# A 90-degree rotation of an 8192 x 8192 matrix: twelve macro tiles as a loop, another buffer rotation, another split of the copies

## The chip, the cores and the metric

The kernel runs on one core of one Trainium2 chip. The metric is the device time of one execution in microseconds: the median over several runs. Profiles come from one further execution, taken by the hardware profiler; its span runs from the first to the last instruction.

## The reference: what is computed

```python
def setup_inputs():
    return {"x": np.random.randn(8192, 8192).astype(np.float32), "k": 1}

def reference(x, k):
    return np.rot90(x, k)
```

With k = 1, out[i, r] = x[r, 8191 - i]: a transposition with the order of the columns reversed. 268 MB are read and 268 MB are written, and nothing is calculated.

## The kernel before, in words

**Tiles.** The matrix is cut into KK = 16 macro tiles of R = 1024 rows by W = 4096 columns. A macro tile is read in T = 8 loads of 128 rows (2 MB each; load m is tile t = m % 8 of macro tile kk = m // 8), and written in J = 8 stores of 2 MB (output n is chunk j = n % 8 of macro tile kk = n // 8). So there are 128 loads and 128 outputs.

**Buffers.** Five buffers of 2 MB: LAND = 2 take turns for landing loads, OUTS = 3 for outputs (`out_buf`, lines 161 to 168). Between them stands `ring`, which holds one macro tile. Load n + 8 overwrites the places in the ring that output n was read from.

**Stages of one period.** SP issues the loads (`by_sync`). VectorE *turns* each landed load (`by_vector`, line 359): it writes it into the ring with reversed columns, the chunks that TensorE will transpose by a plain copy, the others by a transpose of 32 x 32 blocks. An output is then made in one of two ways. By TensorE (`by_pe`, lines 84 to 87: chunks 0 and 4 of most macro tiles, all chunks of the first and the last): 32 transposes into PSUM, in three parts, and ScalarE copies the parts to the output buffer (line 449). Or as a *moved* output: the sixteen 32-row pieces (`pairs`, line 264) are copied from the ring to their places by three engines: VectorE the first BY_DVE = 1 (line 341), GpSimd the next BY_POOL = 9 (line 324), ScalarE the last 6 (lines 430 and 439). 81 outputs are moved. ScalarE issues all the stores (line 457).

**What sets the order.** Every engine's program is written out by hand and runs straight through; semaphores tie them together:
- `room_for(wait, n)`: whoever writes output n waits until the last store from the same output buffer has landed. For a TensorE output it is TensorE that waits, before the last transpose of the first part (line 404).
- VectorE, before it turns load m, makes its piece of output m - 8 (line 340), waits for the load, and then for `s_pool` (GpSimd has made its last piece of output m - 8, line 346) or `s_half` (TensorE has transposed it, line 348).
- GpSimd waits for ScalarE's pieces before its eighth copy of an output and for VectorE's before its ninth (line 320), so that its last copy tells that the output is whole; ScalarE waits for that and issues the store (line 441).
- `taken`: a landing buffer is free when its load has been turned, and for the last load of a macro tile when TensorE has transposed the corner too (line 393; that stands after the second part of chunk 0).

Of the kernel before, what the change touches and what calls it, by code (L numbers as in the profile page):

```python
# [6 lines left out]
P = 128  # L7
# [6 lines left out]
J = W // (G * P)  # L14
# [5 lines left out]
SLOTS = T * J - 1  # L20

Q = 32
BY_DVE = 1
BY_POOL = 9
BY_PE = [0, 4]
EARLY = range(T + 2)
# [5 lines left out]
LAND = 2  # L32
OUTS = 3

LINE = 1024
HEAD = 224


def whole_reads(nc):

    for fn in nc.m.functions:
        for block in fn.blocks:
            for n, ins in enumerate(block.instructions):
                if not isinstance(ins, mybir.InstDMACopy):
                    continue
                src = ins.ins[0]
                ap = [list(d) for d in src.ap]
                if len(ap) == 3 and ap[2][0] == 1 and ap[1][0] == ap[2][1]:
                    ap = [ap[0], [1, 1], [1, ap[1][1] * ap[2][1]]]
                    block.instructions[n] = copy.replace(  # L50
                        ins,
                        ins=[copy.replace(src, ap=ap)],
                        ant_dge_precooked=False,
                    )


def slot(kk, t, j):
# [4 lines left out]
def kernel(tc: tile.TileContext, x: bass.AP, k: bass.AP, out: bass.AP):  # L62
# [93 lines left out]
    def load_buf(m):  # L156
        if m < T:
            return m % (LAND + OUTS)
        return LAND + 2 if m == T else (m - T - 1) % LAND

    def out_buf(n):
        e = n - (KK * J - J)
        if e < 0:
            return LAND + (n + 1) % OUTS
        ends = [load_buf(n_load - 2)]
        ends += [LAND + (KK * J - J + i + 1) % OUTS for i in range(OUTS)]
        ends += [load_buf(n_load - 1)]
        return ends[e % len(ends)]

    def once(e):  # L170
        seen = {}

        def wait(sem, n):
            if seen.get(sem, 0) < n:
                seen[sem] = n
                e.wait_ge(sem, n)

        return wait
# [51 lines left out]
    def at(v, first, dims):  # L230
        return bass.AP(
            tensor=v.tensor, offset=v[:, first : first + 1].offset, ap=[v.ap[0], *dims]
        )
# [29 lines left out]

    pairs = [(a, q) for a in range(P // Q) for q in range(P // Q)]

    def load(e, m):
        r0, c0 = macros[m // T]
        b = load_buf(m)
        rows = slice(0, P)
        if m in BOTH:  # L270
            rows = slice(0 if e is nc.sync else 1, P, 2)
        r = r0 + m % T * P
        e.dma_start(  # L273
            out=bufs[b][rows, :], in_=x[r : r + P, c0 : c0 + W][rows, :]
        ).then_inc(s_land[b], 16)

    def queues(m):
        if m in BOTH:
            return [nc.sync, nc.scalar]
        return [nc.scalar if m in EARLY and m % 2 else nc.sync]  # L280

    def load_in_turn(e, m):
        if e not in queues(m):
            return
        last = [i for i in range(m) if load_buf(i) == load_buf(m)]
        taken(e.wait_ge, last[-1])
        load(e, m)

    def landings(m):
        return 16 * sum(1 + (i in BOTH) for i in range(m + 1) if load_buf(i) == load_buf(m))  # L290
# [5 lines left out]
    with tc.tile_critical():  # L296
        for m in range(LAND + OUTS):
            for e in queues(m):
                load(e, m)
    tc.close()  # L300
    tc.compile()  # L301

    def by_gpsimd(e):
        e.memset(ident, 0.0).then_inc(s_id, 1)  # L304
        e.wait_ge(s_id, 1)
        e.affine_select(  # L306
            out=ident,
            in_=ident,
            compare_op=mybir.AluOpType.not_equal,
            fill=1.0,  # L310
            base=0,
            pattern=[[-1, P]],
            channel_multiplier=1,
        ).then_inc(s_id, 1)
        wait = once(e)
        for n, (kk, _, js, _) in enumerate(outs):
            if moved[n]:
                room_for(wait, n)
                wait(s_rev, turned_in(n))
                others = {BY_POOL - 2: s_act, BY_POOL - 1: s_dve}  # L320
                for c, (to, of) in enumerate(moves(n, pairs[BY_DVE : BY_DVE + BY_POOL])):
                    if c in others:
                        wait(others[c], moved_until(n))
                    i = e.tensor_copy(out=to, in_=of)  # L324
                i.then_inc(s_pool, 1)

    def by_sync(e):
        for m in range(LAND + OUTS, n_load):
            load_in_turn(e, m)

    def by_vector(e):
        wait = once(e)
        for m in range(n_load):
            kk, t = divmod(m, T)
            b = load_buf(m)
            n = m - T
            if n >= 0 and moved[n]:
                room_for(wait, n)
                wait(s_rev, turned_in(n))
                for to, of in moves(n, pairs[:BY_DVE]):  # L340
                    i = e.tensor_copy(out=to, in_=of)  # L341
                i.then_inc(s_dve, 1)
            e.wait_ge(s_land[b], landings(m))
            if n >= 0:
                if moved[n]:
                    e.wait_ge(s_pool, moved_until(n))  # L346
                else:
                    e.wait_ge(s_half, turned_until(n))
            for js in pieces[m]:
                if (m, js[0]) == (n_load - 1, J - 1):  # L350
                    e.wait_ge(s_half, turned_until(KK * J - J))
                if kk < KK - 1 and (t, js[0]) == (T - 1, J - 1):
                    wait(s_rev, rev[m, 0])
                    e.tensor_copy(  # L354
                        out=at(bufs[b][:], 0, [[CH, 1], [1, CH]]), in_=landed(b, js)
                    ).then_inc(s_rev, 1)
                    continue
                turn = e.transpose if in_quadrants(kk, js[0]) else e.tensor_copy
                turn(out=chunk(kk, t, js), in_=landed(b, js)).then_inc(s_rev, 1)  # L359
# [10 lines left out]
                yield n, parts[n]  # L370

    def by_tensor(e):
        wait = once(e)
        e.wait_ge(s_id, 2)
        used = {}
        for n, some in in_turn():
            kk, ts, js, blocks = outs[n]
            rows = len(ts) * P
            order = [(part, f) for part in some for f in part[2]]
            if js[0] == 0 and kk < KK - 1:  # L380
                late = parts[n][-1]
                order.sort(key=lambda o: (o[0] == late, o[1] % rows, o[1]))
            last = dict(order)
            for part, f in order:
                _, h, cols = part
                j, off = blocks[f // rows]
                t = ts[f % rows // P]
                if kk < KK - 1 and js[0] == 0 and f == parts[n][-1][2][0]:
                    m = kk * T + T - 1
                    wait(s_rev, rev[m, J - 1])  # L390
                    wait(s_freed, kk)
                    for g in range(G):
                        i = e.transpose(  # L393
                            corner[:, g * P : g * P + P],
                            bufs[load_buf(m)][:, g * P : g * P + P],
                            ident,
                        )
                    i.then_inc(s_corner, 1)
                if n == KK * J - J and h:
                    wait(s_freed, KK - 1)  # L400
                if used.get(h, part) != part:
                    wait(s_ev, evicted[used[h][0]] + 1)
                wait(s_rev, rev[kk * T + t, j])
                if part == parts[n][0] and f == last[part] and n != FIRST[1]:
                    room_for(wait, n)
                to = cols.index(f) * P
                i = e.transpose(  # L407
                    ps[h][:, to : to + P],
                    chunk(kk, t, [j])[:, 0, off : off + P],
                    ident,  # L410
                )
                if f == last[part]:
                    i.then_inc(s_half, 1)
                    used[h] = part

    def by_scalar(e):
        wait = once(e)
        e.wait_ge(s_id, 2)
        e.copy(scratch, ident[:, :1])  # L419
        for m in EARLY[LAND + OUTS :]:  # L420
            load_in_turn(e, m)
        for n, (kk, ts, js, blocks) in enumerate(outs):
            r0, c0 = macros[kk]
            rows = len(ts) * P
            b = out_buf(n)
# [16 lines left out]
            else:  # L442
                for k, h, cols in parts[n]:
# [11 lines left out]
            top = M - c0 - js[0] * CH - groups * P  # L455
            left = r0 + ts[0] * P
            e.dma_start(  # L457
                out=out[top : top + groups * P, left : left + rows].rearrange(
                    "(g m) f -> m g f", m=P
                ),  # L460
                in_=bufs[b][:, : groups * rows].rearrange("m (g f) -> m g f", f=rows),
            ).then_inc(s_store[b], 16)

    by_gpsimd(nc.gpsimd)
    by_sync(nc.sync)
    by_vector(nc.vector)
    by_tensor(nc.tensor)
    by_scalar(nc.scalar)

    last = {out_buf(n): n for n in range(n_out)}  # L470
    for b in sorted(last, key=last.get):
# [36 lines left out]
```

## Time and profile before

| what | value |
|---|---|
| time, median of 3 runs | 1258.23 us (1258.2 to 1258.35) |
| span of the profiled execution | 1256.9 us |
| HBM read, written | 268.44 MB, 268.44 MB |
| busy: GpSimd, ScalarE, VectorE, TensorE | 805.0, 682.5, 612.7, 330.0 us |
| store, issue to landing (median) | 18.6 us |
| load from SP, issue to landing (median) | 15.2 us |

The profiled execution's own time is its span of 1256.9 us; the median of the timed runs lies 1.33 us above it. How to read it: each engine has a row of busy time, and the DMA engines have a row of their own with the rate in GB/s for 40 equal slices of the span. A group of instructions is told as "line engine operation out<-in shape xcount | busy us, mean ns | idle before it and what ended the idle time"; the engines are PE (TensorE), DVE (VectorE), ACT (ScalarE), POOL (GpSimd) and SP. The queues q1 and q10 carry loads and stores, q8 and q14 carry instructions.

### The profile page before, as it was taken

What the parts mean: (1) busy time and instruction counts of PE and PEld (TensorE: products, weight loads), DVE (VectorE), ACT (ScalarE), POOL (GpSimd) and SP (SyncE); (2) the same over time, 40 slices, a digit from 0 to 9 for tenths busy, and PEclk for the clock granted to TensorE, in tenths of its full rate; (3) what the DMA queues carried; (4) which work ended last, traced back from release to release, by engine and by line L of the source; (5) the groups of instructions that cost most, each with busy time, mean ns of one, the idle gap of its engine ahead of it and who ended that gap; (6) DMA issues with size and microseconds to landing.
All of it is one profiled execution on the core that took longest, in us unless ns stands there. A gap on an engine that the chain in (4) does not pass through costs nothing.

```text
span 1256.9 us, 5389 instructions
## 1 busy us (share of the span) xinstructions
PE 330.0 (26%) x1556; PEld 267.9 (21%) x1556; DVE 612.7 (49%) x373; ACT 682.5 (54%) x637; POOL 805.0 (64%) x735
## 2 busy tenths in 40 slices
PE   1555122221122211222212322023220232214374
PEld 0444111211112110121201212012120121103364
DVE  2544554556545555455555555555555555453310
ACT  0334565565555655566555555556555655556454
POOL 0000886768867679677797767977678776795500
PEclk9987555555555555565555555555555555555588
DMA  9999999999999999999999999999999999999999
GB/s 398 420 431 428 430 428 430 430 430 430 428 429 430 430 429 428 430 429 430 429 430 429 430 427 431 430 430 429 430 429 430 429 429 429 429 430 429 430 426 394
DMA packets 36957, 537.22 MB, mean 427 GB/s; under 512 B 4160, under 2 KB 4160, under 8 KB 4160
## 3 DMA queue, kind: packets, MB, share of 16 engines
q10 hardware_dynamic: 19184, 278.93, 52.2%
q1 hardware_dynamic: 17744, 257.96, 48.0%
q8 instruction: 12, 0.20, 0.1%
q14 instruction: 17, 0.14, 0.0%
HBM read 268.44 MB, written 268.44 MB: 427 GB/s over the span
## 4 chain that ended last, share of the span: by engine, by line
DMA 72%; DVE 16%; POOL 5%; ACT 3%; issue 2%; PE 1%; ACTq 0%; SPq 0%; DVEq 0%
DMA buf<-in_x_dram 65%; DVE ring L359 16%; DMA out_dram<-buf 7%; POOL buf L324 5%; ACT buf L449 3%; PE ps L407 1%; ACTq L457 0%; DVE buf L341 0%; PE ps L393 0%; SPq L273 0%; DVE buf L354 0%; DVEq L346 0%; SPq L301 0%; SPq L193 0%; SPq L296 0%
## 5 line engine op out<-in xcount | busy, mean ns | idle before, releaser
L324 POOL COPY buf<-ring 32x1024 f32<-32x1024 f32 (+1 forms) x729 | 804.3, 1103 | 380.3 <-DMA out_dram<-buf 343.4
L407 PE MATMUL ps<-head,ring 128*128 128x128 f32 x1496 | 316.8, 384 | 880.6 <-DVE ring L359 430.3
L407 PEld LDWEIGHTS ps<-head,ring 128*128 128x128 f32 x1496 | 257.6, 200 | 936.9 <-DVE ring L359 435.0
L359 DVE COPY ring<-buf 128x1024 f32<-128x1024 f32 (+5 forms) x152 | 158.1, 1047 | 599.3 <-DMA buf<-in_x_dram 578.1
L439 ACT COPY buf<-ring 32x1024 f32<-32x1024 f32 (+1 forms) x405 | 414.8, 1024 | 4.9
L359 DVE STREAM_TRANSPOSE ring<-buf 128x3072 f32<-128x3072 f32 (+2 forms) x125 | 357.8, 2870 | 0.0
L449 ACT COPY buf<-ps 128x2048 f32<-128x2048 f32 (+1 forms) x134 | 174.6, 1355 | 251.8 <-PE ps L407 177.1
L430 ACT COPY buf<-ring 32x1024 f32<-32x1024 f32 x81 | 82.9, 1024 | 291.6 <-POOL buf L324 229.9
L341 DVE COPY buf<-ring 32x1024 f32<-32x1024 f32 x81 | 108.0, 1334 | 0.0
L393 PE MATMUL ps<-head,buf 128*128 128x128 f32 x60 | 16.2, 424 | 30.3 <-DVE buf L354 30.3
L393 PEld LDWEIGHTS ps<-head,buf 128*128 128x128 f32 x60 | 10.6, 213 | 35.7 <-DVE buf L354 35.7
L433 ACT COPY buf<-ps 128x512 f32<-128x512 f32 x15 | 8.8, 586 | 8.9 <-DMA out_dram<-buf 8.8
L354 DVE COPY buf<-buf 128x512 f32<-128x512 f32 x15 | 5.8, 388 | 0.0
L419 ACT ACT_TABLE_LOAD x1 | 1.3, 1283 | 3.4 <-PEq L301 3.4
L304 POOL MEMSET head<- 128x128 f32 x1 | 0.2, 205 | 2.9 <-POOLq L301 2.9
L306 POOL TENSOR_SCALAR_AFFINE_SELECT head<-head 128x128 f32<-128x128 f32 x1 | 0.3, 292 | 0.2 <-POOL head L304 0.2
L489 POOL MEMSET const-float32-0.0<- 128x1 f32 x1 | 0.1, 98 | 0.2 <-issue 0.2
L419 ACT COPY head<-head 128x1 f32<-128x1 f32 x1 | 0.2, 192 | 0.0
L489 POOL MEMSET const-bfloat16-1.0<- 128x1 bf16 x1 | 0.1, 100 | 0.0
L489 POOL MEMSET const-uint8-127<- 128x1 uint8 x1 | 0.1, 100 | 0.0
L489 POOL MEMSET const-float32-1.0<- 128x1 f32 x1 | 0.1, 98 | 0.0
## 6 DMA issues: line engine op xcount, KB each, us to landing
out_dram<-buf ACTq DMA_DIRECT2D x128, 2048.0 KB, 18.6
buf<-in_x_dram SPq DMA_DIRECT2D x121, 2048.0 KB, 15.2
buf<-in_x_dram ACTq DMA_DIRECT2D x3, 2048.0 KB, 17.3
buf<-in_x_dram SPq DMA_DIRECT2D x4, 1024.0 KB, 16.1
buf<-in_x_dram ACTq DMA_DIRECT2D x4, 1024.0 KB, 16.5
```

Of the source, the lines that this page charges most:

```text
L324: i = e.tensor_copy(out=to, in_=of)
L341: i = e.tensor_copy(out=to, in_=of)
L354: e.tensor_copy(out=at(bufs[b][:], 0, [[CH, 1], [1, CH]]), in_=landed(b, js)).then_inc(s_rev, 1)
L359: turn(out=chunk(kk, t, js), in_=landed(b, js)).then_inc(s_rev, 1)
L393: i = e.transpose(corner[:, g * P : g * P + P], bufs[load_buf(m)][:, g * P : g * P + P], ident,)
L407: i = e.transpose(ps[h][:, to : to + P], chunk(kk, t, [j])[:, 0, off : off + P], ident,)
L419: e.copy(scratch, ident[:, :1])
L430: e.copy(to, of)
L433: e.copy(at(bufs[b][:], rows - P, [[rows, G], [1, P]]), at(corner, 0, [[P, G], [1, P]]),).then_inc(s_freed, 1)
L439: i = e.copy(to, of)
L449: e.copy(at(bufs[b][:], cols[0], [[rows, deep], [1, run]]), at(ps[h][:], 0, [[run, deep], [1, run]]),).then_inc(s_ev, 1)
L489: nc = _bacc.Bacc("TRN2", target_bir_lowering=False, num_devices=1)
```

## The change

Three constants and tables change. VectorE makes the first 3 of the 16 pieces of a moved output and ScalarE the last 4, where it was 1 and 6; GpSimd keeps 9, but others than before. The output buffer of output n comes from the table TURN, which repeats after sixteen outputs, and no longer from (n + 1) % 3, which would not repeat with an even number of macro tiles. Within a macro tile a buffer still comes back after three outputs; where two macro tiles meet, the first output of the new one gets the buffer of two outputs before, and the second that of four before.

The rest puts twelve macro tiles into loops. Each engine's program is first recorded (`Program`, `Op`, `Place`) and then played: GpSimd plays macro tiles 1 to 12, VectorE and TensorE 2 to 13, as six turns of two macro tiles each, and the others straight through. ScalarE and SP have no loop. In a loop each wait takes its value from a register that moves on with the turn; GpSimd also has an instruction of its own (`sem_inc`) behind each group of waits. [...]

```diff
-BY_DVE = 1
+BY_DVE = 3
 BY_POOL = 9
...
+TURN = [[1, 2, 0, 1, 2, 0, 1, 2], [1, 0, 2, 1, 0, 2, 1, 0]]
...
+class Op:
...
+    def run(self, e, shift=0, value=None):
+        if self.name == "wait_ge":
+            e.wait_ge(self.args[0], self.args[1] if value is None else value)
+            return
+        kwargs = {k: v.at(shift) if isinstance(v, Place) else v for k, v in self.kwargs.items()}
+        i = getattr(e, self.name)(*self.args, **kwargs)
+        if self.inc:
+            i.then_inc(*self.inc)
...
+class Program:
...
+    def play(self, nc, e, first=None, times=0, slot=0):
+
+        span = range(first, first + 2 * times) if times else range(0)
+        for kk, ops in self.parts.items():
+            if kk not in span:
+                for op in ops:
+                    op.run(e)
+            elif kk == first:
+                self.loop(nc, e, first, times, slot)
+
+    def loop(self, nc, e, first, times, slot):
+        turns = [
+            [op for kk in (first + 2 * i, first + 2 * i + 1) for op in self.parts[kk]]
+            for i in range(times)
+        ]
...
+        with nc.Fori(1, times + 1, engines=[e.engine], head_slot={e.engine: slot}) as i:
+            passed = nc.alloc_semaphore("passed") if e is nc.gpsimd else None
+            waited = False
+            for ops in zip(*turns):
+                op = ops[0]
+                if waited and op.name != "wait_ge" and passed is not None:
+                    e.sem_inc(passed, 1)
+                waited = op.name == "wait_ge"
+                if op.name == "wait_ge":
+                    n = [o.args[1] for o in ops]
+                    step = n[1] - n[0]
...
+                    op.run(e, value=i * step + (n[0] - step) if step else n[0])
+                    continue
...
+                else:
+                    op.run(e)
...
         if e < 0:
-            return LAND + (n + 1) % OUTS
+            return LAND + TURN[n // J % 2][n % J]
         ends = [load_buf(n_load - 2)]
-        ends += [LAND + (KK * J - J + i + 1) % OUTS for i in range(OUTS)]
+        ends += [LAND + i for i in range(OUTS)]
         ends += [load_buf(n_load - 1)]
...
     def by_gpsimd(e):
+        e.part(-1)
...
         for n, (kk, _, js, _) in enumerate(outs):
+            e.part(kk)
...
-    by_gpsimd(nc.gpsimd)
     by_sync(nc.sync)
-    by_vector(nc.vector)
-    by_tensor(nc.tensor)
-    by_scalar(nc.scalar)
+    for e, by, first, times in (
+        (nc.gpsimd, by_gpsimd, 1, 6),
+        (nc.vector, by_vector, 2, 6),
+        (nc.tensor, by_tensor, 2, 6),
+        (nc.scalar, by_scalar, None, 0),
+    ):
+        program = Program()
+        by(program)
+        program.play(nc, e, first, times)
```

`by_vector`, `by_tensor` and `by_scalar` get the same `e.part(kk)`, and the store's target becomes a `Place`, which a loop could shift. The loads' order and their queues stay as they were.

More of the change, by code (lines that the diff above doesn't have):

```diff
@@ L54, in whole_reads, with __init__, at, key @@
                     )
+class Place:
+    def __init__(self, out, top, rows, left, cols):
+        self.out, self.top, self.rows, self.left, self.cols = out, top, rows, left, cols
+    def at(self, shift):
+        cols = bass.ds(self.left + shift, self.cols)
+        return self.out[self.top : self.top + self.rows, cols].rearrange(
+            "(g m) f -> m g f", m=P
+        )
+    def key(self):
+        return (self.top, self.rows, self.cols)
+def key_of(v):
+    if isinstance(v, bass.AP):
+        return (v.tensor.name, v.offset, str(list(v.ap)))
+    if isinstance(v, Place):
+        return v.key()
+    return str(v)
@@ new lines, with __init__, then_inc, key @@
+class Op:
+    def __init__(self, name, args, kwargs):
+        self.name, self.args, self.kwargs, self.inc = name, args, kwargs, None
+    def then_inc(self, sem, n=1):
+        assert self.inc is None
+        self.inc = (sem, n)
+    def key(self):
+        if self.name == "wait_ge":
+            return (self.name, str(self.args[0]))
+        named = sorted((k, key_of(v)) for k, v in self.kwargs.items())
+        return (self.name, [key_of(v) for v in self.args], named, str(self.inc))
+    def run(self, e, shift=0, value=None):
+        if self.name == "wait_ge":
+            e.wait_ge(self.args[0], self.args[1] if value is None else value)
[4 more added lines that the diff above has]
+            i.then_inc(*self.inc)
@@ new lines, with __init__, part, __getattr__ @@
+class Program:
+    def __init__(self):
+        self.parts, self.now = {}, None
+    def part(self, kk):
+        self.now = self.parts.setdefault(kk, [])
+    def __getattr__(self, name):
+        def record(*args, **kwargs):
+            op = Op(name, args, kwargs)
+            self.now.append(op)
+            return op
+        return record
+    def play(self, nc, e, first=None, times=0, slot=0):
[11 more added lines that the diff above has]
+        ]
+        for i, ops in enumerate(turns):
+            assert len(ops) == len(turns[0]), (str(e.engine), i, len(ops), len(turns[0]))
+            for a, b in zip(ops, turns[0]):
+                assert a.key() == b.key(), (str(e.engine), i, a.key(), b.key())
+        with nc.Fori(1, times + 1, engines=[e.engine], head_slot={e.engine: slot}) as i:
[9 more added lines that the diff above has]
+                    step = n[1] - n[0]
+                    assert n == [n[0] + k * step for k in range(times)]
+                    assert n[0] > 0 and step >= 0
+                    op.run(e, value=i * step + (n[0] - step) if step else n[0])
+                    continue
+                left = [v.left for o in ops for v in o.kwargs.values() if isinstance(v, Place)]
+                if left:
+                    step = left[1] - left[0]
+                    assert left == [left[0] + k * step for k in range(times)]
+                    op.run(e, shift=i * step - step)
+                else:
+                    op.run(e)
@@ L264, with load @@
     pairs = [(a, q) for a in range(P // Q) for q in range(P // Q)]
-    def load(e, m):
+    def load(e, m, queue):
         r0, c0 = macros[m // T]
@@ L270, in load @@
         if m in BOTH:
-            rows = slice(0 if e is nc.sync else 1, P, 2)
+            rows = slice(0 if queue is nc.sync else 1, P, 2)
         r = r0 + m % T * P
@@ L280, in queues, with load_in_turn @@
         return [nc.scalar if m in EARLY and m % 2 else nc.sync]
-    def load_in_turn(e, m):
-        if e not in queues(m):
+    def load_in_turn(e, m, queue):
+        if queue not in queues(m):
             return
@@ L286, in load_in_turn @@
         taken(e.wait_ge, last[-1])
-        load(e, m)
+        load(e, m, queue)
     def landings(m):
@@ L298 @@
             for e in queues(m):
-                load(e, m)
+                load(e, m, e)
     tc.close()
@@ L328, in by_sync @@
         for m in range(LAND + OUTS, n_load):
-            load_in_turn(e, m)
+            load_in_turn(e, m, nc.sync)
     def by_vector(e):
@@ L334, in by_vector @@
             kk, t = divmod(m, T)
+            e.part(kk)
             b = load_buf(m)
@@ L372, in by_tensor @@
     def by_tensor(e):
+        e.part(-1)
         wait = once(e)
@@ L377, in by_tensor @@
             kk, ts, js, blocks = outs[n]
+            e.part(kk)
             rows = len(ts) * P
@@ L416, in by_scalar @@
     def by_scalar(e):
+        e.part(-1)
         wait = once(e)
@@ L420, in by_scalar @@
         for m in EARLY[LAND + OUTS :]:
-            load_in_turn(e, m)
+            load_in_turn(e, m, nc.scalar)
         for n, (kk, ts, js, blocks) in enumerate(outs):
+            e.part(kk)
             r0, c0 = macros[kk]
@@ L457, in by_scalar @@
             e.dma_start(
-                out=out[top : top + groups * P, left : left + rows].rearrange(
-                    "(g m) f -> m g f", m=P
-                ),
+                out=Place(out, top, groups * P, left, rows),
                 in_=bufs[b][:, : groups * rows].rearrange("m (g f) -> m g f", f=rows),
             ).then_inc(s_store[b], 16)
-    by_gpsimd(nc.gpsimd)
     by_sync(nc.sync)
-    by_vector(nc.vector)
-    by_tensor(nc.tensor)
-    by_scalar(nc.scalar)
+    for e, by, first, times in (
[7 more added lines that the diff above has]
+        program.play(nc, e, first, times)
     last = {out_buf(n): n for n in range(n_out)}
```

## The prediction

> **What bounds the kernel now.** I read four views, in this order: the page's DMA rows, the answer by stretches of time, the timeline of one macro tile, and the trace's records of DMA completions.
>
> The page first: the span, the rate of the DMA engines in 40 slices, and the queues.
>
> ```profile
> span 1256.9 us, 5389 instructions
> ...
> DMA  9999999999999999999999999999999999999999
> GB/s 398 420 431 428 430 428 430 430 430 430 428 429 430 430 429 428 430 429 430 429 430 429 430 427 431 430 430 429 430 429 430 429 429 429 429 430 429 430 426 394
> ...
> q8 instruction: 12, 0.20, 0.1%
> q14 instruction: 17, 0.14, 0.0%
> ```
>
> The reader is to see that the rate stands at 428 to 431 GB/s in every slice but the first two and the last two. The sixteen DMA engines are full; no other engine is (GpSimd 64%, ScalarE 54%, VectorE 49%). The last two rows are code being fetched: 12 packets of 16 KB and 17 of 8 KB, over the same DMA engines.
>
> The stretches (length, busy time of the five engine rows with counts, clock, DMA share, GB/s):
>
> ```profile
> 200.00:1000.00 800.00, 169.07 (x691) 133.41 (x689) 427.49 (x256) 461.46 (x442) 605.96 (x557) 0.52 1.01 429
> ...
> 1250.00:1252.00 2.00, 0.00 (x0) 0.00 (x0) 0.00 (x0) 0.00 (x0) 0.00 (x0) 0.50 0.98 418
> 1252.00:1254.00 2.00, 0.00 (x0) 0.00 (x0) 0.00 (x0) 0.00 (x0) 0.00 (x0) 0.50 0.89 377
> 1254.00:1256.00 2.00, 0.00 (x0) 0.00 (x0) 0.00 (x0) 0.00 (x0) 0.00 (x0) 0.50 0.39 164
> ```
>
> For 800 us there is no gap at all. At the end the rate crumbles: some DMA engines are done, others not. The completion records say it exactly: the sixteen parts of the last store land between 1253.41 and 1256.85 us, at these distances from the first: four below 0.2, four at 1.1 to 1.3, five at 2.4 to 3.0, three at 3.3 to 3.44. Their sum is 28.8 us.
>
> Where does the lag come from? After the first TensorE code fetch (60.2 us) one part of the store landing at 63.97 is 1.4 us behind the other fifteen. If a 16 KB fetch costs its DMA engine 1.4 us and an 8 KB fetch half, 12 x 1.4 + 17 x 0.7 = 28.7 us: the lags of the last store. So I hold **code fetches** to be what spreads the engines, and the slowest engine (3.44 us) to set the end.
>
> Last, a stretch of the timeline (start, length, instruction; idle before it):
>
> ```profile
> 824.37 8.93 POOL L324 COPY buf<-ring 32x1024 f32<-32x1024 f32 x8 [8.67 <-DMA out_dram<-buf]
> ...
> 828.04 1.13 DVE L359 COPY ring<-buf 128x1024 f32<-128x1024 f32 x1 [5.88 <-DMA buf<-in_x_dram]
> 829.10 3.36 DVE L359 STREAM_TRANSPOSE ring<-buf 128x3072 f32<-128x3072 f32 x1
> 832.39 1.45 DVE L341 COPY buf<-ring 32x1024 f32<-32x1024 f32 x1
> 833.90 22.05 POOL L324 COPY buf<-ring 32x1024 f32<-32x1024 f32 x19 [0.61 <-DVE buf L341]
> ```
>
> VectorE turns a load the moment it lands (every 9.76 us), then makes its one piece; GpSimd's ninth copy waits for that piece. GpSimd starts an output when the store three back has landed.
>
> **The change, part by part.** The profiled execution has 1256.9 us of span; the runs' median is 1258.23, 1.33 us more. I carry every difference over to the median.
>
> *Less code.* Fetched bytes per instruction are 12 x 16,384 / 3,148 = 62 on TensorE, 17 x 8,192 / 2,241 = 62 on the other four. The built code falls on TensorE from 1,556 transposes (two instructions each) to 876, with 53 others: 1,805 instructions, 7 fetches; on the other four from 2,252 to 1,307 instructions, 10 fetches. That leaves 7 x 1.4 + 10 x 0.7 = 16.8 of 28.7 us, 59%, if a loop's body stays in the instruction memory. If the slowest engine's lag shrinks alike, 3.44 to 2.0: **-1.4 us**. Ends: 0 (its fetches are the early ones and ScalarE's, which stay) and -3.44 (it loses all). I take -1.3, nearer the proportion than either end.
>
> [...]
>
> *Two pieces go from ScalarE to VectorE.* ScalarE saves 2 x 1.04 us per moved output, beside its idle time: 0. VectorE pays at most 2 x 1.41 (row L341, 32x1024) = 2.8 us; over 81 outputs 228 us, 613 to 841 of 1257. The single records show that GpSimd's copy takes 1.03 us alone and 1.40 when it begins under a VectorE copy, so GpSimd pays up to 2 x 0.37 more. The order decides: VectorE makes the pieces of output n after the turn of load n+7 and before that of n+8, and that turn waits for GpSimd's ninth copy, which now waits for three pieces. I walk one triple of moved outputs (1 to 3 of macro tile 10; loads land at 828.02, 837.78, 847.53, 857.30):
> - Output 1: turn ends 832.6, three pieces by about 835.3, ninth copy 836.4; next turn on time at 837.8.
> - Output 2: GpSimd from 836.4, eight copies (8 x 1.074) plus four collisions x 0.37 until 846.5; pieces done 846.4; ninth copy 847.6; turn on time (+0.1).
> - Output 3: from 847.6, eight copies until 857.7, ninth 858.75; the turn of the load of 857.30 is 1.4 us late.
> Then comes a TensorE output: no pieces, and VectorE waits for a load again (5.8 us idle now), so the lag is gone. What a late turn delays is the load two on: today it is issued at 861.33, 5.7 us before the load ahead of it lands (867.05); 4.3 stay. Stores of the triple go out up to 2.8 us later, and the store ahead lands 7.4 to 9.6 us after today's issue. Both DMA queues stay fed: **0**. Without that cover each lost microsecond would cost 28 (two triples in 14 macro tiles).
>
> *Sixteen-step rotation.* The first output of a macro tile gets the buffer used two outputs before, not three; the second gets one used four before. At macro tile 10: the store two back lands at 824.32, while today the first output is issued at 824.51. TensorE's last transpose of its first half now waits until 824.32; behind it stand the corner transposes (so the freeing of a landing buffer) and the late part. ScalarE then needs 1.87 + 1.45 us, the third copy 0.6: issue about 828.9, 4.4 us later; the store ahead lands at 834.08, so 5 us of cover stay. The load that the corner frees is issued 826.5 instead of 823.08; the one ahead lands at 828.02. The load queue may thin out for a moment, but the store queue then gets the engines' whole rate: **0**, and with the cover gone up to 3 us in each of 14 macro tiles. SP's waits are the same; all its loads follow VectorE and the corner.
>
> *Loop instructions.* 34 register instructions a turn on VectorE, 31 on TensorE, 21 on GpSimd, one compare-and-branch each; no row shows any. Ends: 0.02 us (a wait instruction's record on VectorE) and 0.55 us (a DMA issue, the dearest on a sequencer). At the dear end 34 x 0.55 = 19 us per turn of 156 us, where VectorE keeps some 52 idle; at the near end 0.7. I take the near end, 0. The back edges come where the engine waits anyway: TensorE 25 us, GpSimd 8.7, VectorE 5.8.
>
> Sum: -1.3 us. 1258.23 - 1.3 = **1256.9**.
>
> **Rivals.**
> 1. *The loops fetch their code again in each turn.* TensorE's body is 136 transposes and 35 others, 307 instructions, more than one 16 KB block; GpSimd's 170 is more than one 8 KB block. Two blocks each, six turns: 12 x 1.4 + 12 x 0.7 = 25 us more on sixteen engines; 42 us in all against 28.7, so the slowest lags 3.44 x 42 / 28.7 = 5.0 instead of 3.44. Price +1.6: **1259.8**. [...]
> 2. *The slowest DMA engine keeps its fetches.* The change then shows nothing: **1258.2**.
> 3. *The slowest engine loses nearly all of them*, for most of the fetches between 300 and 1060 us go: 1258.23 - 3 = **1255.2**.
> 4. *The other side: VectorE's cycle grows past the load's 9.76 us.* Place: the triples of moved outputs. Turn 4.4 + pieces 4.3 + ninth copy 1.05 is 9.75, at the edge; GpSimd's own 11.1 is over it, and only the TensorE outputs make up for it. It decides from a lag of about 4.3 us at the third turn, three times what I find; each microsecond over it then costs up to 28, and with half a microsecond **1272**. Against it: ScalarE's and GpSimd's idle, and that stores fill in for late loads.
>
> That the change does not do what it says shows as rival 1.
>
> **How the numbers follow.** A measurement of this kernel can tell about 0.2%, 2.5 us, from no change. Forecast (1255.8 to 1257.9) 0.56; rival 1, 0.14; rival 2, 0.12; rival 3, 0.06; rival 4, 0.12. The forecast and rivals 1 and 2 lie within 2.5 us: 0.82; so does a third of rival 3 (0.02), and I move 0.03 of rival 1 to slower for what lies past 1260.7. Same 0.81, faster 0.04, slower 0.15. Range 1255.2 to 1260.0: it leaves out rival 4 and the far ends of rivals 1 and 3, some 0.19.
>
> **What would show it.** Fewer code packets (about 7 and 10) and a spread of the last store's landings near 2 us: the first step right. The same or more packets: rival 1. A rate below 425 GB/s in the middle slices: rival 4, or the rotation. VectorE busy near 800 us and GpSimd's mean copy near 1.17 us would bear out the second step; a first output issued some 4 us later in its macro tile, the third. I would be wrong if lateness of the pieces adds up over macro tiles rather than clearing at each TensorE output.

## The result and the profile after

The changed kernel takes **1261.82 us** (median of 6 runs, 1259.79 to 1263.61) against 1258.22 us of the kernel before, run beside it (1258.08 to 1258.35): a ratio of 1.0029, 95% interval 1.0018 to 1.0041. It is 3.6 us slower, where I forecast 1.3 us faster, and it lies outside my range. The profiled execution is one of 1261.52 us with a span of 1260.2 us. The runs of the kernel before agree within 0.3 us; those of the changed kernel spread over 3.8.

The page of the changed kernel: span, DMA rate in 40 slices, and the two rows of code fetches (packets, MB, share of the sixteen DMA engines).

```profile
span 1260.2 us, 6055 instructions
...
GB/s 398 421 428 424 413 431 428 430 431 428 431 430 428 430 431 428 430 429 427 425 430 429 429 428 426 431 428 428 431 430 429 428 429 426 431 429 421 430 426 393
...
q8 instruction: 7, 0.11, 0.0%
q14 instruction: 13, 0.11, 0.0%
```

The reader is to see two things. The fetches fell from 29 to 20 (7 of TensorE's and 13 others; I had said 7 and 10). And the row that stood at 428 to 431 has holes: 413 in the fifth slice, 424 to 427 here and there, 421 near the end. The DMA engines are no longer always fed.

The stretches of the changed kernel (start and end, length, busy time of PE, PEld, DVE, ACT, POOL with counts, clock, DMA share, GB/s) show the deepest hole, and the end:

```profile
118.00:124.00 6.00, 1.54 (x6) 1.14 (x6) 0.00 (x0) 1.11 (x1) 4.95 (x5) 0.50 1.01 427
124.00:132.00 8.00, 4.58 (x19) 3.78 (x19) 5.91 (x5) 6.75 (x7) 0.43 (x1) 0.62 0.99 344
...
1254.00:1256.00 2.00, 0.00 (x0) 0.00 (x0) 0.00 (x0) 0.00 (x0) 0.00 (x0) 0.50 0.98 418
1256.00:1258.00 2.00, 0.00 (x0) 0.00 (x0) 0.00 (x0) 0.00 (x0) 0.00 (x0) 0.50 0.79 336
1258.00:1260.00 2.00, 0.00 (x0) 0.00 (x0) 0.00 (x0) 0.00 (x0) 0.00 (x0) 0.50 0.08 33
```

Between 124 and 132 us the rate is 344 GB/s. The same stretch of the kernel before has 428:

```profile
124.00:132.00 8.00, 0.00 (x0) 0.00 (x0) 3.78 (x2) 4.76 (x5) 7.67 (x9) 0.55 1.00 428
```

The end is steeper: the sixteen parts of the last store land within 2.49 us (3.44 before), and their distances from the first add up to 12.6 us (28.8 before).

I add up the lost rate from the trace's DMA packets: in steps of 2 us, the part by which the rate is under 429.5 GB/s, times the step (a step above it counts against).

| lost, us | 100 to 200 | 200 to 1000 | 1000 to 1210 |
|---|---|---|---|
| before | 0.10 | 0.08 | 0.08 |
| after | 1.63 | 1.23 | 0.88 |

That is 3.5 us more, and the span is 3.3 us longer. The steeper end gives nothing back: the sixteen parts of the last store land 3.2 us later in the mean, and the last of them 3.3 us later. The first border, where macro tile 0 ends and 1 begins, costs 1.5 us alone. Here is that place in the timeline (start, length, instruction; idle before it). Before:

```profile
117.02 9.74 SPq L273 DMA_DIRECT2D buf<-in_x_dram  x2
...
118.02 0.55 ACTq L457 DMA_DIRECT2D out_dram<-buf  x1
...
122.43 0.69 DVE L359 COPY ring<-buf 128x1024 f32<-128x1024 f32 x1 [5.88 <-DMA buf<-in_x_dram]
```

After:

```profile
122.38 0.69 PE L102 MATMUL ps<-head,ring 128*128 128x128 f32 x2 [8.27 <-DMA out_dram<-buf]
...
122.86 1.06 PE L102 MATMUL ps<-head,buf 128*128 128x128 f32 x4
122.89 3.70 ACT L102 COPY buf<-ps 128x2048 f32<-128x2048 f32 x3 [15.37 <-PE ps L102]
124.01 6.29 SPq L383 DMA_DIRECT2D buf<-in_x_dram  x2
...
125.96 0.69 DVE L102 COPY ring<-buf 128x1024 f32<-128x1024 f32 x1 [8.03 <-PE ps L102]
...
126.61 0.55 ACTq L102 DMA_DIRECT2D out_dram<-buf  x1
```

TensorE waits 8.27 us for a store to land. Only then come the four corner transposes (the `ps<-head,buf` row), and only then SP's load: 124.01 instead of 117.02. The load ahead of it landed at 122.90, so the load queue was empty; of the stores one was in flight. The first store of the macro tile goes out at 126.61 instead of 118.02.

The packets of the two queues show where the rate goes. From 122 to 125 us the store queue alone carries 421 GB/s. Its one store ends at 126.89, and although the next is issued at 126.61, its first packet moves at 131.24. Between 127 and 131 us the late load is alone, at 360 GB/s and falling as its sixteen parts run out.

### The profile page after: what moved, and what is told of

The parts are those of the page before. It is cut to its first block, busy times and chain, and to the rows that moved or that the text cites. A ratio compares the mean times of both kernels' runs of the same rounds, so it can differ in the third digit from the quotient of the medians.

```text
span 1260.2 us, 6055 instructions
## 1 busy us (share of the span) xinstructions
PE 329.3 (26%) x1556; PEld 265.7 (21%) x1556; DVE 785.6 (62%) x535; ACT 513.8 (41%) x475; POOL 819.4 (65%) x735
## 4 chain that ended last, share of the span: by engine, by line
DMA 60%; DVE 20%; POOL 8%; issue 4%; ACT 3%; PE 2%; ACTq 0%; DVEq 0%; POOLq 0%; SPq 0%
DMA buf<-in_x_dram 44%; DMA out_dram<-buf 16%; DVE ring L102 14%; POOL buf L102 8%; DVE buf L102 6%; ACT buf L102 3%; PE ps L102 2%; ACTq L102 0%; DVEq L99 0%; POOLq L99 0%; SPq L383 0%; POOLq L149 0%; SPq L303 0%; SPq L411 0%; SPq L406 0%
## 5 line engine op out<-in xcount | busy, mean ns | idle before, releaser
L102 POOL COPY buf<-ring 32x1024 f32<-32x1024 f32 (+1 forms) x729 | 818.7, 1123 | 369.7 <-DVE ring L102 143.0
L102 ACT COPY buf<-ring 32x1024 f32<-32x1024 f32 x324 | 332.0, 1025 | 366.1 <-POOL buf L102 339.3
L102 PEld LDWEIGHTS ps<-head,ring 128*128 128x128 f32 x1496 | 252.9, 198 | 978.1 <-DVE ring L102 419.9
L102 DVE COPY ring<-buf 128x1024 f32<-128x1024 f32 (+5 forms) x152 | 165.8, 1097 | 428.0 <-DMA buf<-in_x_dram 360.1
L102 ACT COPY buf<-ps 128x2048 f32<-128x2048 f32 (+4 forms) x149 | 181.6, 1278 | 362.9 <-PE ps L102 241.3
L102 DVE COPY buf<-ring 32x1024 f32<-32x1024 f32 (+1 forms) x243 | 272.6, 1122 | 2.2
```

Of the source, the lines that this page charges most:

```text
L102: i = getattr(e, self.name)(*self.args, **kwargs)
```

## The experiments

Three theories: **R**, the rotation (the first output of a macro tile waits for the store two back); **P**, VectorE's three pieces; **L**, the loops' own instructions. A cycle is the time from the issue of one output's store to that of the next. All times are medians, beside runs of the kernel before on the same chip.

| kernel | us | before | ratio, 95% |
|---|---|---|---|
| e1, three pieces alone | 1259.19 | 1258.24 | 1.0007 (0.9998 to 1.0016) |
| e2, rotation alone | 1261.38 | 1258.24 | 1.0027 (1.0016 to 1.0038) |
| e3, no loops | 1262.30 | 1258.24 | 1.0035 (1.0021 to 1.0049) |
| e4, loops, rotation, one piece | 1261.10 | 1258.24 | 1.0022 (1.0012 to 1.0031) |
| e5, first and last border free | 1259.10 | 1258.27 | 1.0006 (0.9997 to 1.0015) |
| e6, the same, one piece | 1259.43 | 1258.27 | 1.0009 (1.0000 to 1.0018) |
| e7, loops of six macro tiles | 1261.22 | 1258.27 | 1.0024 (1.0015 to 1.0034) |
| e8, rotation, ScalarE waits | 1258.26 | 1258.27 | 1.0000 (0.9991 to 1.0009) |
| e9, changed kernel, ScalarE waits | 1258.78 | 1258.19 | 1.0003 (0.9989 to 1.0017) |
| e10, the same, one piece | 1258.52 | 1258.19 | 1.0002 (0.9987 to 1.0016) |
| e11, more code on SP | 1286.07 | 1258.19 | 1.0221 (1.0202 to 1.0240) |
| e12, more code on ScalarE | 1263.28 | 1258.22 | 1.0040 (1.0025 to 1.0055) |
| e13, more code on TensorE | 1261.94 | 1258.22 | 1.0030 (1.0018 to 1.0041) |
| e14, more code on GpSimd | 1262.18 | 1258.22 | 1.0032 (1.0020 to 1.0044) |

**One part at a time (e1 to e4).**

```diff
-BY_DVE = 1
+BY_DVE = 3
```

> The kernel before with one edit: VectorE makes 3 of the 16 pieces, ScalarE 4; straight programs, the old rotation. Theory P (the pieces: a moved output's cycle grows from 10.4 to about 11.8 us and the cover of the DMA queues runs out): 1260 to 1262 us. Theory R (the rotation: the first output of a macro tile waits for the store two back): 1258 to 1259. Theory L (the loops' register instructions, waits and branches): 1258.2, as before, with a cycle near 10.4.

1259.19, 0.95 us over before and short of theory P's 1260: a part, not the whole. (The interval just includes no change, but all eleven runs, from 1258.86, lie above the 23 of before, up to 1258.62.) The cycle did grow, if less than P says (11.5 us from output 1 to output 2, 10.5 before). But from 200 to 1000 us it lost only 0.33 us of DMA rate; 1.1 us went between 1100 and 1110, among the outputs of macro tile 13, while VectorE turns the loads of macro tile 14:

```profile
1100.00:1110.00 10.00, 3.72 (x20) 3.43 (x19) 8.19 (x6) 4.89 (x6) 9.36 (x8) 0.67 1.00 378
```

378 GB/s, with VectorE busy 8.19 us of 10 and GpSimd 9.36.

```diff
+TURN = [[1, 2, 0, 1, 2, 0, 1, 2], [1, 0, 2, 1, 0, 2, 1, 0]]
...
-            return LAND + (n + 1) % OUTS
+            return LAND + TURN[n // J % 2][n % J]
...
-        ends += [LAND + (KK * J - J + i + 1) % OUTS for i in range(OUTS)]
+        ends += [LAND + i for i in range(OUTS)]
```

> The kernel before with one edit: the output buffers rotate by the sixteen-step table; straight programs, one piece by VectorE. Theory P: 1258.2. Theory R: 1260 to 1262, with the first store of a macro tile some 4 us or more later than before and dips in the DMA rate there. Theory L: 1258.2.

1261.38: theory R. The rotation alone costs 3.14 us.

```diff
-        (nc.gpsimd, by_gpsimd, 1, 6),
-        (nc.vector, by_vector, 2, 6),
-        (nc.tensor, by_tensor, 2, 6),
+        (nc.gpsimd, by_gpsimd, None, 0),
+        (nc.vector, by_vector, None, 0),
+        (nc.tensor, by_tensor, None, 0),
```

> The changed kernel with its three loops played straight through; three pieces and the new rotation stay. Theories P and R: as slow as the changed kernel or slower by the code that is fetched again, 1261.8 to 1263.2. Theory L: about 1258 to 1259, and the cycle of a moved output goes from 11.8 back to about 10.4 us.

1262.30: theories P and R. The cycle from output 1 to output 2 is 11.78 us, with loops 11.84: the register waits cost nothing that can be seen. Rotation and pieces add up, 3.14 + 0.95 = 4.09 where this kernel has 4.06 over before. That the loops then give 0.48 back is not shown: the runs of this kernel spread over 2.2 us, those of the changed one over 3.8.

```diff
-BY_DVE = 3
+BY_DVE = 1
```

> The changed kernel with one piece by VectorE and six by ScalarE; loops and rotation stay. Theory P: the fewer fetches show, 1256.9 to 1257.6. Theory R: 1260 to 1261.5. Theory L: 1260.5 to 1262, with cycles of moved outputs longer than the 10.4 us of before.

Applied to the changed kernel: 1261.10, theory R. The time would fit theory L too, but L asks for longer cycles, and output 1 to 2 takes 10.5 us as before.

**Where the short distance costs (e5, e6).** In the changed kernel the first outputs of the macro tiles 1 to 14 wait for the store two back, so there are fourteen borders with a short distance (not fifteen, as my expectation of e5 counts). What lies outside a loop may choose its buffers freely: e5 and e6 free the first border, 0 to 1, and the last, 13 to 14.

```diff
-TURN = [[1, 2, 0, 1, 2, 0, 1, 2], [1, 0, 2, 1, 0, 2, 1, 0]]
+TURN = [[0, 2, 1, 0, 2, 1, 0, 2], [0, 1, 2, 0, 1, 2, 0, 1]]
+ENDS = {0: [1, 2, 0, 1, 2, 0, 1, 2], 14: [2, 0, 1, 2, 0, 1, 2, 0]}
...
-            return LAND + TURN[n // J % 2][n % J]
+            return LAND + ENDS.get(n // J, TURN[n // J % 2])[n % J]
...
-        ends += [LAND + i for i in range(OUTS)]
+        ends += [LAND + (i + 1) % OUTS for i in range(OUTS)]
```

> The changed kernel, loops and three pieces kept, but the short distance of the rotation is gone at the two borders that lie outside what the loops must repeat: from macro tile 0 to 1, and from 13 to 14. Theory R in the form that the first border (1.5 us of DMA rate lost between 124 and 134 us) and the last one carry most: about 1259.5 to 1260. Theory that every border costs alike: 15 borders become 13, so 1261.3 to 1261.6.

1259.10: with three pieces, 2.7 of the 3.6 us come from two borders of fourteen, more than I expected.

> The same with one piece by VectorE. First and last border carry it: 1258 to 1259, between the kernel before and 1 us over it. Every border alike: 1260.5 to 1260.9. If the code that is no longer fetched sets the end as I forecast, it comes in under 1258.2.

1259.43, above the 1258 to 1259 of the first theory, and far from the 1260.5 of the other; with one piece the two borders make 1.7 of the 2.9 us (e4 to e6). It loses nothing at the first border, but 0.6 us of rate at the next, which keeps the short distance, and 0.9 us after 1210 (0.4 before). It isn't under 1258.2, so it shows no gain from the fewer fetches.

**Loops without the rotation (e7).** Two turns of six macro tiles, which a rotation of three fits.

```diff
-TURN = [[1, 2, 0, 1, 2, 0, 1, 2], [1, 0, 2, 1, 0, 2, 1, 0]]
+PER = 6
...
-            [op for kk in (first + 2 * i, first + 2 * i + 1) for op in self.parts[kk]]
+            [op for kk in range(first + PER * i, first + PER * i + PER) for op in self.parts[kk]]
...
-            return LAND + TURN[n // J % 2][n % J]
+            return LAND + (n + 1) % OUTS
...
-        (nc.gpsimd, by_gpsimd, 1, 6),
-        (nc.vector, by_vector, 2, 6),
-        (nc.tensor, by_tensor, 2, 6),
+        (nc.gpsimd, by_gpsimd, 1, 2),
+        (nc.vector, by_vector, 2, 2),
+        (nc.tensor, by_tensor, 2, 2),
```

> Loops of two turns of six macro tiles on the three engines, which the old rotation of three fits; one piece by VectorE. It keeps the loops and takes away both other parts. Theory R: as fast as before, and a little faster if fewer fetches count: 1257.2 to 1258.2. Theory that the loops themselves cost: over 1259.5.

1261.22: a miss. Its body on GpSimd is 496 instructions (170 in the changed kernel), and the 8 KB fetches are 22, more than the 17 of the straight program: three of them stand at 583 to 589 us, right behind the branches back of GpSimd (579.9) and VectorE (584.4), which I read as loop code fetched again. One part of its last store lands 1.95 us behind the second last. No experiment takes e7's 3 us apart; I take them for fetches.

**What hangs on the wait (e8).** The rotation alone as in e2, but the wait for the buffer moves from TensorE to ScalarE.

```diff
-                if part == parts[n][0] and f == last[part] and n != FIRST[1]:
+                if part == parts[n][0] and f == last[part] and n != FIRST[1] and (kk == KK - 1 or js[0]):
                     room_for(wait, n)
...
-            if moved[n] or n == FIRST[1] or (kk < KK - 1 and js[0] == J - 1):
+            if moved[n] or n == FIRST[1] or (kk < KK - 1 and js[0] in (0, J - 1)):
                 room_for(wait, n)
```

> The kernel with the new rotation alone, but for the first output of a macro tile ScalarE waits for the output buffer before its copies, and TensorE does not, so the corner (and the landing buffer that it frees) no longer stands behind the store two back. If the lost time comes through the corner and the load behind it: 1258.5 to 1259.5. If it comes through the late part (VectorE's next turn waits for TensorE's third part, that for ScalarE's first copy, that for the store) and the late store: 1260.5 to 1261.5, as with the rotation alone.

1258.26, as before: **all** of the rotation's cost is gone, more than the theory of the corner asked for. The timeline at the first border, e2 and then e8:

```profile
123.71 6.36 SPq L275 DMA_DIRECT2D buf<-in_x_dram  x2
...
126.31 0.55 ACTq L459 DMA_DIRECT2D out_dram<-buf  x1
```

```profile
116.04 1.11 PE L395 MATMUL ps<-head,buf 128*128 128x128 f32 x4 [2.60 <-DVE buf L356]
117.25 12.42 SPq L275 DMA_DIRECT2D buf<-in_x_dram  x2
122.19 3.70 ACT L451 COPY buf<-ps 128x2048 f32<-128x2048 f32 x3 [14.58 <-DMA out_dram<-buf]
...
125.92 0.55 ACTq L459 DMA_DIRECT2D out_dram<-buf  x1
```

The store goes out nearly as late as in e2 (125.92 against 126.31). Only the corner, and with it the load, is early again: 117.25 against 123.71. The stretch from 124 to 132 us, first e2, then e8:

```profile
124.00:132.00 8.00, 4.29 (x19) 3.67 (x19) 4.54 (x3) 7.33 (x8) 0.00 (x0) 0.68 1.02 358
```

```profile
124.00:132.00 8.00, 4.58 (x19) 3.78 (x19) 4.54 (x3) 7.33 (x9) 0.00 (x0) 0.67 1.02 433
```

358 GB/s with the late load, 433 with the early one. The late load is the cause of the rotation's cost: with the store as late, and the load early, nothing is lost. A late load with an early store was not run.

**The same mend in the changed kernel (e9, e10).**

> The changed kernel, but for the first output of a macro tile ScalarE waits for the output buffer and TensorE does not; loops, three pieces and the sixteen-step rotation stay. If the corner behind that wait is what the changed kernel lost to: about 1258 to 1259 (what three pieces cost alone, 0.9 us over before, less what the fewer code fetches give). If the loops or the pieces cost by themselves in this company: over 1260.

1258.78, as expected: 3.0 of the changed kernel's 3.6 us are gone.

> The same with one piece by VectorE: only the loops and a rotation that no longer blocks the corner are left. Theory of the code fetches (they spread the DMA engines, 28.8 us of lag in all, 3.4 on the slowest): lag near 17 us in all and 2 on the slowest, 1256.5 to 1257.5. Theory that the lag does not set the end, or that loops cost: 1258.2 or more.

1258.52. Here only the loops are left of the change and a rotation that no longer holds up the corner, and no DMA rate is lost between 100 and 1210 us. The fetches are 21. Yet the kernel is not faster: the lags of the last store add up to 25.5 us, and the slowest is at 4.35, later than the 3.44 of the kernel before. My theory of the fetches falls here in the form in which I had it.

**What a code fetch costs, and whom (e11 to e14).** Each adds waits for a semaphore reached long ago, so that the code grows and the work doesn't.

```diff
             load_in_turn(e, m)
+            for _ in range(64):
+                e.wait_ge(s_id, 1)
```

> The kernel before with 64 more waits behind each of SP's 121 later loads, all for a semaphore that was reached long ago; built, they are 32 instructions a load, some 3,870 in all, which makes some 30 more code fetches of 8 KB and nothing else (SP waits for a buffer there anyway). Theory of the code fetches at 0.7 us of one DMA engine each: 21 us more lag in all, 49 instead of 28.8, and the slowest engine 1.3 us (by the mean) to 2.5 us (by its own share) later: 1259.5 to 1260.8. If the fetches are hidden: 1258.2.

1286.07: far above both. The DMA rows show 31 more fetches, 0.25 MB:

```profile
q14 instruction: 48, 0.39, 0.1%
```

28 us for 31 fetches is 0.9 us each, although one moves 8 KB by one of sixteen DMA engines, in a packet of 0.31 us. SP still sat waiting for VectorE 914 us in all, so its issues were not held up. The completion records show where the time goes: of the store that landed at 996.82 us fourteen parts lie within 0.61 us, one at 1.27 and one at 11.7. **One** part is far behind; the rate dips every 40 us, the period of SP's fetches. I take it that one DMA engine is late and that everything waits for it. (A record of a landing doesn't name the engine; that it is the same one throughout is my reading of a single part being late from landing to landing.)

```diff
             ).then_inc(s_store[b], 16)
+            for _ in range(16):
+                e.wait_ge(s_id, 1)
```

> The kernel before with 16 more waits (8 instructions, for a semaphore reached long ago) behind each store that ScalarE issues: 1,024 instructions, 8 more code fetches of 8 KB. Theory PINNED (an engine's code is always fetched by the same DMA engine, so that one falls behind; SP's extra code cost 28 us over some 30 fetches, 0.95 us each): 1262 to 1266. Theory SPREAD (fetches go round the sixteen DMA engines): 8 x 0.95 / 16 = 0.5 us, 1258.2 to 1259.2.

1263.28, PINNED: 5.1 us for 8 fetches, and again one straggler (9.0 us at 1102.62, the next 2.36). A caution: the eight instructions hold ScalarE for 0.58 us after a store in the median, and for 0.9 at 601.93 (the store takes 0.55, the next copy starts at 603.42), so not all of the 5.1 need be fetches.

```diff
             order = [(part, f) for part in some for f in part[2]]
...
                 if f == last[part]:
                     i.then_inc(s_half, 1)
                     used[h] = part
+            if 0 < kk < KK - 2 and js[0] == 4:
+                for _ in range(512):
+                    e.wait_ge(s_id, 1)
```

> The kernel before with 512 more waits (256 instructions) on TensorE behind output 4 of the macro tiles 1 to 13, where it waits 25 us for a store anyway: 3,328 instructions, 13 more code fetches of 16 KB. PINNED: 13 x 1.4 = 18 us on one DMA engine, 1270 to 1276. SPREAD: 18 / 16 = 1.1 us, 1258.5 to 1260.

1261.94, between the two, nearer to SPREAD: 3.7 us for 13 fetches, twice the bytes each. The added waits don't fall into an idle time of 25 us, as I had said: they take 27 us, and TensorE makes up the small transposes of the next macro tile behind them, still ahead of the corner.

```profile
q8 instruction: 25, 0.41, 0.1%
```

Many parts are late here, not one: of the store that landed at 1101.48 four lie within 0.14 us and twelve between 3.8 and 9.6.

```diff
                 i.then_inc(s_pool, 1)
+                if js[0] in (3, 7):
+                    for _ in range(64):
+                        e.wait_ge(s_id, 1)
```

> The kernel before with 64 more waits (32 instructions) on GpSimd behind outputs 3 and 7 of each macro tile with moved outputs, ahead of its idle time: 864 instructions, some 7 more code fetches of 8 KB. PINNED: 7 x 0.95 = 6.6 us, 1261.5 to 1265. SPREAD: 0.4 us, 1258.2 to 1259.

1262.18, PINNED: 4.0 us for 7 fetches, one straggler (9.49 us at 1102.92, the next 4.52).

A loop on ScalarE, which would take most of its fetches away, was not run. No kernel of this study beats the kernel before; e8 equals it.

## Why the prediction was wrong

**The rotation: the failed step.** I priced it "**0**", since "the load queue may thin out for a moment, but the store queue then gets the engines' whole rate". It cost 3.1 us alone. I had the mechanism whole, the corner behind TensorE's wait and the load behind the corner, and then took both covers (what is still queued ahead) from one border, at macro tile 10: a load 1.5 us ahead of the landing before it, and 5 us of stores. There I was nearly right: the load came 2.1 us ahead, and only 0.1 us of rate was lost. At the first border neither cover was there. The load came 1.1 us after that landing (124.01 against 122.90). The store queue did get the whole rate, 421 GB/s, but had one store left; the next was issued 0.7 us before that one landed (126.61 against 127.34), not 5, and its first packet moved 4.6 us after its issue. So both queues ran dry in turn, and the rate fell to 344 GB/s. (A slice under 425 GB/s was the sign that I had named: the fourth and the fifth have 424 and 413.) Over the borders of the changed kernel the trace has 1.6 us lost at the first, 0.6 at the last, 0.5 and 0.4 at those to macro tiles 7 and 9, and 0.13 at most at each other. The late store did no harm in e8 (1258.26 us), where the load was early.

**The pieces.** My walk was near on the cycle: 11.2 and 11.15 us by it, 11.5 and 11.2 in e1 (11.8 and 11.3 in the changed kernel). In the changed kernel VectorE's turn waits for GpSimd where it waited for the load:

```profile
620.35 4.33 DVE L102 COPY buf<-ring 32x1024 f32<-32x1024 f32 x3
...
626.70 0.69 DVE L102 COPY ring<-buf 128x1024 f32<-128x1024 f32 x1 [2.01 <-POOL buf L102]
```

The three pieces take the 4.3 us that I had put, and the lag clears at the TensorE output, as I said. But I walked macro tile 10 alone. Among the outputs of macro tile 13, while VectorE turns the loads of macro tile 14, the lag grows: in e1 a load is issued at 1099.78, 2.0 us ahead of the landing before it (6.3 in the kernel before), where my walk left 4.3. That cover gives out: 1.1 us. "0" should have been 0.9.

**The code fetches.** The forecast "-1.3" shows as no gain that is clear of noise: -0.5 (e3 to the changed kernel), +0.3 (e8 to e10). The count was right, the reasoning was not. I took the lags of the last store, 28.8 us, for the sum of all fetches. That they agree was luck: in the kernel before, the lags of a landing between 1050 and 1150 us add up to 43 us in the median, and fall again to 28.8. And I scaled the slowest engine's lag by the number of all fetches, as if they went round the DMA engines. Those of SP, ScalarE and GpSimd seem to pile up on one DMA engine each (one part 11.7, 9.0 and 9.49 us late in e11, e12 and e14); only TensorE's look spread (e13: twelve parts 3.8 to 9.6 us late). In e10 the lags between 1050 and 1150 us are smaller, 30 us, as fewer fetches would have it, but the slowest part of the end is not. ScalarE has no loop, so what its fetches put on one DMA engine would stay; by that reading this is rival 2, which I gave 0.12, but no run takes ScalarE's fetches away. Which engine's code sits on the slowest DMA engine of the kernel before, and why e10's slowest is later still, stays open. What e11 measured is 0.9 us a fetch, paid by the data transfers and not by SP, which still sat waiting for VectorE 914 us.

My sign for this step was wrong too. A spread of 2.49 us looks like the forecast, but e1 and e3, with all their fetches, have 2.09 and 1.91. In e1 the late parts caught up where the DMA rate fell: the lags of a landing add up to 36 us ahead of the hole at 1100 us (378 GB/s) and to 16 behind it. A shorter spread showed the loss, not the gain.

**Rival 1** did not happen: 20 fetches, none of TensorE's between 285.7 and 1173.1 us, so TensorE's body was not fetched again in each turn. e7, with bodies three times as long, shows 8 KB fetches behind the branch back, but none of TensorE's between 552.9 and 1143.3 us, though its body is 917 instructions there. **Rival 4** had the right sign and the right kind, DMA queues that run dry, at the wrong place. **The loop's instructions** cost nothing that shows, as I had it: a cycle of 11.84 us with loops, 11.78 without.

## What to carry to other kernels

When a kernel is bound by DMA, ask of every wait that you move what is queued behind it on the same engine, and whether a load's issue hangs on that; here a late store alone cost nothing (e8, 1258.26 us), and a late load together with it cost it all (e2, 1261.38). Check the cover at the borders of the schedule, not only in its middle, and for both queues at once: here two borders of fourteen made more than half of the loss (2.7 of 3.6 us with three pieces, 1.7 of 2.9 with one). And let the engine wait that has nothing else to release: moving one wait from TensorE to ScalarE took the rotation's whole cost away (1261.38 to 1258.26 us).

## What the runs showed of the hardware

- The store queue alone carried nearly the whole rate while it had work: 421 GB/s from 122 to 125 us in the changed kernel, against 429 with both from 200 to 1000 us. The gap came between its last transfer and the next: a store issued into the emptying queue moved its first packet 4.2 to 4.6 us later at the first border (changed kernel, e2, e3, e4).
- More code on one engine slowed the transfers: 31 more fetches of 8 KB by SP cost 28 us, and one part of a transfer came up to 12.5 us behind the first, which I read as one DMA engine that makes all of SP's fetches. TensorE's 13 more fetches of 16 KB cost 0.29 us each, and twelve of sixteen parts were late.
- A wait long fulfilled was not free on the two engines where it was timed: in e12 such instructions follow each other on ScalarE every 0.077 us, twice the 0.038 us of their records; in e13 some 256 of them take TensorE 27 us, 0.105 us each.
- GpSimd's copy of 32 x 1024 elements takes 1.03 us in most cases, and 1.40 when VectorE copies at the same time; a VectorE copy of that shape begun under a GpSimd copy ends 0.55 us after that one's end (0.90 to 1.51 us in all). With three pieces GpSimd's mean rose from 1.12 to 1.13 us only; it now waits 74 us for VectorE's pieces, 7 before, so I take it that VectorE works partly in those waits.
